# Hybrid attention block: the four single-purpose PSUM banks become one pool of four

## The chip, the cores and the metric

The kernel runs on one core of one Trainium2 chip. The metric is the device time of one launch in microseconds (us). TensorE (PE) does matrix products and transposes, PEld is its weight load, VectorE is DVE, ScalarE is ACT, GpSimd is POOL, and SyncE (SP) issues all loads.

## The reference

Two layers of a block run over 256 tokens of the stream x (width 1024) beside 256 context tokens. Each layer computes, from a normalised and modulated input h = norm(x)*(1+scale)+shift:

```python
p  = h @ w_in                               # keys, values, queries, gates, ...
y_na  = neighbourhood_attention(q, k, v, k_ctx, v_ctx, rpb)   # 8 heads of 64, bias table, mask
y_gm  = spatial_gating(gelu(u), gelu(v), ...)
y_mla = dense_attention(q_mla, [k_ctx; k_mla], [v_ctx; v_mla])  # 8 heads of 96, values of 64
y  = g0*(y_na @ na_w_o) + g1*(y_gm @ gm_w_o) + g2*(y_mla @ mla_w_o)  # g = sigmoid(p's gates)
x  = x + gt1 * (y @ w_out)
x  = x + gt2 * squared_relu_mlp(norm(x)*(1+scale)+shift)
```

In layer 0 the context tokens go through the same block (their attention sees context alone); in layer 1 only x does. The modulation vectors (shift, scale, gt) come from a product of a condition vector with w_mod.

## The kernel before

Activations lie transposed, 128 features by up to 512 tokens (256 of x, 256 of context; layer 1 works on 256). Every large product is made of three: weights and activations are each split into a rounded part and a rest (`split1`, L113, casts on ACT and subtracts on DVE), and `mm3` (L287 to L289) multiplies high by high, low by high and high by low into one PSUM tile.

PSUM has eight banks of 128 x 512 float32, and every PSUM tile is a whole bank. The function `psum` (L47) gives it a tag, and a tag owns a number of banks: "mm" four (all large products: `b_ps`, `gate`, `z`, `u`, `kv`, `qm`, `o_ps`, `f`), "s" two, "pt" one, "pv" one. What uses the last three:

- "s": the attention scores `S`, the transposes of keys and queries (`tr_ps`, `c_tr`, `h_tr`), the spatial gating product `sg`, and small ones (`st_ps`, `mod_t`, `rsum`).
- "pt": the transposed probabilities `pt`, and the sums of the modulation (`mod_ps` of `mod_quarter` and one of two in `mod_pooled`).
- "pv": the products of probabilities and values `pv` and `pvm`, the broadcast of the norms `rstd_b`, and the second sum of `mod_pooled`.

Attention is `soft_pv` (L427). It runs for four pairs of heads `j`, and in each for one or two streams and two blocks of 128 queries. For a block it forms the scores of both heads (two tiles `S`), then for each head: bias (DVE, neighbourhood attention on x only), row maximum (DVE, L445), exponential with its sum (ACT, L448, into one of two SBUF tiles `P`), reciprocal and scaling (DVE, L450, L451), transposes into `pt` (PE, L454) and a copy to SBUF (ACT, L456). After both blocks the products with the values go to `pv` (L460), which stays until `split_out` has read it (L423, L424), after all streams of the pair.

The order of the work is found when the program is built. A planner simulates the engines; each engine takes the ready instruction with the highest priority, which is its place in the program text, moved forward where `high_priority` says so. An instruction that writes a new tile can only be taken when a buffer of the tile's tag is free. The order so found is fixed: on the chip each engine works its list off from front to back and waits where an input or a buffer is late.

To give PE work beside the softmax, products of `gate` and `z` are spread over it. Each score product is recorded in `marks`, and `paced` (L305) lets the i-th group of three products (one `mm3`) go into the list only behind the score product that its share names, with the first `FREE` = 10 or `FREE2` = 36 groups free. Neighbourhood attention spreads 4 chunks of 12 groups in layer 0 and 6 in layer 1; the dense attention (MLA) spreads 96 groups.

Of the kernel before, what the change touches and what calls it, by code (L numbers as in the profile page):

```python
# [7 lines left out]
F32 = mybir.dt.float32  # L8
# [18 lines left out]
def hybrid_block_kernel(tc, a, out):  # L27
# [3 lines left out]
    mm = nc.tensor.matmul  # L31

    from contextlib import ExitStack, nullcontext
    with ExitStack() as es:
        def pool(name, bufs=1, **kw):
            return es.enter_context(tc.tile_pool(name=name, bufs=bufs, **kw))
# [8 lines left out]
        pp = pool("ps", space=PSUM)  # L45

        def psum(tag, name):  # L47
            return pp.tile([128, 512], F32, tag=tag, name=name, bufs={"mm": 4, "s": 2, "pt": 1, "pv": 1}[tag])


        def g2(name, dt=F32R):
# [88 lines left out]
        def mod_finish(ps, w, dsts, modT, bmod, streams):  # L140

            t = tmp2("mod_sb")
            vec.tensor_copy(t[:, :w], ps[:, :w])
            pst = psum("s", "mod_t")
            for i in range(w // 128):
                nc.tensor.transpose(pst[:, i * 128:(i + 1) * 128], t[:, i * 128:(i + 1) * 128], ident)
            for i in range(w // 128):
                v4 = pst[:, i * 128:(i + 1) * 128].rearrange("p (j r) -> p j r", j=4)
                for v in range(streams):
                    o, b = dsts(modT[:, v, :], i), dsts(bmod, i)  # L150
                    i0 = v4[:, :, v]
                    if len(o.shape) == 3:
                        i0 = i0.rearrange("p (a b) -> p a b", a=2)
                    vec.tensor_tensor(out=o, in0=i0, in1=b, op=ALU.add)

        def mod_quarter(l, q, modT, bmod, streams):

            ps = psum("pt", "mod_ps")
            for kb in range(4):
                for kk in range(2):  # L160
                    raw = g2("rawm", F32)
                    nc.sync.dma_start(out=raw, in_=a["wmod1"][l, q, kb][:, kk * 512:kk * 512 + 512])
                    mod_cols(ps, raw, 0, 128, 2 * kb + kk)
                yield
            mod_finish(ps, 128, lambda m, i: m[:, 0:16].rearrange("p (a c) -> p a c", a=2)[:, :, 2 * q:2 * q + 2], modT,
                       bmod, streams)

        def mod_group(l, g, modT, bmod, streams):
            ps = psum("mm", "mod_ps")
            for k in range(KC):  # L170
                raw = load(a["wmod"][l, g - 2, k])
                mod_cols(ps, raw, 0, 256, k)
                yield
            mod_finish(ps, 256, lambda m, i: m[:, 8 * g:8 * g + 8].rearrange("p (j i) -> p j i", i=2)[:, :, i], modT, bmod,
                       streams)
# [371 lines left out]
        for l in range(L):  # L547
# [192 lines left out]
            for j in range(4):  # L740
# [6 lines left out]
                pv = psum("pv", "pv")  # L747
# [94 lines left out]
            for j in range(4):  # L842
                pv = psum("pv", "pvm")
# [226 lines left out]
```

## Time and profile before

| | |
|---|---|
| median of 3 runs (lowest, highest) | 1402.77 us (1400.9, 1403.62) |
| profiled execution: time, span | 1402.83 us, 1400.8 us |
| PE busy, weight loads | 1370.2 us (98%), 1161.8 us |
| DVE, ACT, POOL busy | 957.4, 704.7, 56.9 us |
| granted TensorE clock | 1.000 |
| matmuls | 8438 |
| DMA | 210.61 MB, mean 150 GB/s |

The span is the time from the first to the last instruction of the profiled execution; its whole time is 2.03 us longer. Busy is the union of an engine's instructions, so a PE at 98% stands still for 30.6 us in the span. In a row of the timeline the number in square brackets is how long the engine sat idle before the row and what ended that.

### The profile page before, as it was taken

To read this page: it belongs to the slowest core of one execution; us is meant where nothing else is said; L and a number is where in the kernel's file an instruction comes from. 1 tells how busy PE (TensorE), PEld (TensorE's weight loads), DVE (VectorE), ACT (ScalarE), POOL (GpSimd) and SP (SyncE) were. 2 spreads that over 40 slices of the span, in tenths; PEclk is the share of its full clock that TensorE was granted. 3 is DMA by queue.
4 is the path that set the end of the run, shared out by engine and by line. 5 is a ranking of instruction groups with operands and counts; after the bars stand their busy time and mean duration, and the time that the engine had idled before them with its cause. 6 is when DMAs were issued, how large, how long until landed. Compare 5 with 4: busy or idle time off the path is not lost.

```text
span 1400.8 us, 22572 instructions
## 1 busy us (share of the span) xinstructions
PE 1370.2 (98%) x8438; PEld 1161.8 (83%) x8438; DVE 957.4 (68%) x2071; ACT 704.7 (50%) x1440; POOL 56.9 (4%) x35
## 2 busy tenths in 40 slices
PE   6999999999999999999999999999999999999999
PEld 4788767777676789988888888988888878999998
DVE  4666477665563558899766665786787766877775
ACT  3466256443453346623324233566676665656654
POOL 0110000110000000000000000011002100000000
PEclk9999999999999999999999999999999999999999
DMA  9423542234313465665555552443543434566664
GB/s 331 142 84 106 187 150 90 71 105 123 119 46 114 127 195 168 208 202 172 203 205 188 175 197 89 150 137 94 181 136 99 136 91 136 181 181 180 183 183 148
DMA packets 67214, 210.61 MB, mean 150 GB/s; under 512 B 8609, under 2 KB 9633, under 8 KB 67105
## 3 DMA queue, kind: packets, MB, share of 16 engines
q1 hardware_dynamic: 67104, 209.18, 46.6%
q8 instruction: 66, 1.08, 0.3%
q14 instruction: 44, 0.35, 0.1%
HBM read 208.10 MB, written 1.05 MB: 149 GB/s over the span
## 4 chain that ended last, share of the span: by engine, by line
PE 96%; DVE 1%; DMA 1%; ACT 1%; issue 0%; SPq 0%; POOL 0%; ACTq 0%; DVEq 0%
PE o_ps L287 8%; PE o_ps L289 8%; PE o_ps L288 8%; PE f L288 6%; PE f L287 6%; PE f L289 6%; PE gate L287 5%; PE gate L288 5%; PE gate L289 5%; PE b_ps L287 5%; PE b_ps L288 4%; PE b_ps L289 4%; PE pt L454 3%; PE S L417 2%; PE z L287 2%; PE z L289 2%
## 5 line engine op out<-in xcount | busy, mean ns | idle before, releaser
L115 ACT ACTIVATE wh<-raw 128x512 fp32r<-128x512 f32 (+1 forms) x570 | 353.1, 626 | 515.8 <-PE o_ps L288 179.7
L116 DVE TENSOR_TENSOR wl<-raw,wh 128x512 fp32r<-128x512 f32 (+1 forms) x570 | 385.8, 683 | 178.1 <-ACT wh L115 172.7
L289 PE MATMUL f<-hH,wl 128*128 128x258 f32 (+2 forms) x560 | 180.9, 324 | 0.1
L287 PE MATMUL f<-hH,wh 128*128 128x258 f32 (+2 forms) x560 | 180.4, 323 | 0.5 <-ACT wh L115 0.5
L288 PE MATMUL f<-hL,wh 128*128 128x258 f32 (+2 forms) x560 | 180.4, 324 | 0.2 <-DVE hL L277 0.2
L288 PE MATMUL o_ps<-aL,wh 128*128 128x256 f32 (+1 forms) x544 | 176.1, 327 | 0.0
L287 PE MATMUL o_ps<-aH,wh 128*128 128x256 f32 (+1 forms) x544 | 176.0, 328 | 0.0
L289 PE MATMUL o_ps<-aH,wl 128*128 128x256 f32 (+1 forms) x544 | 175.6, 328 | 0.0
L287 PE MATMUL gate<-hH,wh 128*128 128x512 f32 (+1 forms) x384 | 140.5, 366 | 0.0
L289 PE MATMUL gate<-hH,wl 128*128 128x512 f32 (+1 forms) x384 | 130.3, 339 | 0.0
L288 PE MATMUL gate<-hL,wh 128*128 128x512 f32 (+1 forms) x384 | 130.1, 339 | 0.0
L287 PEld LDWEIGHTS f<-hH,wh 128*128 128x128 f32 x560 | 106.0, 190 | 9.1 <-ACT wh L115 0.7
L289 PEld LDWEIGHTS f<-hH,wl 128*128 128x128 f32 x560 | 106.2, 190 | 8.5 <-DVE wl L116 0.3
L288 PEld LDWEIGHTS f<-hL,wh 128*128 128x128 f32 x560 | 105.9, 190 | 8.5 <-DVE hL L277 0.4
L287 PEld LDWEIGHTS o_ps<-aH,wh 128*128 128x128 f32 x544 | 102.7, 190 | 9.5 <-ACT aH L937 0.8
L288 PEld LDWEIGHTS o_ps<-aL,wh 128*128 128x128 f32 x544 | 103.1, 190 | 8.5
L289 PEld LDWEIGHTS o_ps<-aH,wl 128*128 128x128 f32 x544 | 102.7, 190 | 8.8
L288 PE MATMUL b_ps<-wl,hH 128*128 128x512 f32 (+2 forms) x288 | 108.8, 381 | 0.0
L289 PE MATMUL b_ps<-wh,hL 128*128 128x512 f32 (+2 forms) x288 | 106.3, 381 | 0.0
L287 PE MATMUL b_ps<-wh,hH 128*128 128x512 f32 (+2 forms) x288 | 103.7, 385 | 0.0
L200 DVE SCALAR_TENSOR_TENSOR macc<-rawx,sS,macc 128x512 f32<-128x512 f32 x112 | 78.9, 748 | 32.7 <-DMA rawx<-in_wmod_dram 32.4
L287 PEld LDWEIGHTS gate<-hH,wh 128*128 128x128 f32 x384 | 72.7, 189 | 15.9 <-issue 7.5
(229 smaller groups left out, 2481.3 us busy)
## 6 DMA issues: line engine op xcount, KB each, us to landing
raw<-in_wa_dram SPq DMA_DIRECT2D x147, 512.0 KB, 3.6
raw<-in_w_dram SPq DMA_DIRECT2D x68, 512.0 KB, 3.6
raw<-in_wb_dram SPq DMA_DIRECT2D x32, 512.0 KB, 3.3
raw<-in_wmod_dram SPq DMA_DIRECT2D x32, 512.0 KB, 3.4
rawx<-in_wmod_dram SPq DMA_DIRECT2D x32, 512.0 KB, 4.5
raw<-in_wo_dram SPq DMA_DIRECT2D x24, 512.0 KB, 3.6
rawm<-in_wmod_dram SPq DMA_DIRECT2D x32, 256.0 KB, 6.0
rawx<-in_wmod_dram SPq DMA_DIRECT2D x32, 256.0 KB, 4.2
```

What stands on the lines that cost most here:

```text
L115: act(out=wh[:, :width], in_=src, func=AF.Copy)
L116: vec.tensor_tensor(out=wl[:, :width], in0=src, in1=wh[:, :width], op=ALU.subtract)
L200: summed = vec.scalar_tensor_tensor(out=o, in0=src, scalar=s, in1=o, op0=ALU.mult, op1=ALU.add)
L287: mm(ps, lhsT=sh, rhs=mh, start=first, stop=False)
L288: mm(ps, lhsT=sh, rhs=ml, start=False, stop=False)
L289: mm(ps, lhsT=sl, rhs=mh, start=False, stop=last)
L417: return mm(s, lhsT=Q[h][0:96, q0:q0 + 128], rhs=K[h][0:96, k0:k0 + nk], start=True, stop=True)
L454: nc.tensor.transpose(pt[:, i * 128:(i + 1) * 128], P[:, i * 128:(i + 1) * 128], ident)
```

## The change

Every tag other than "mm" is replaced by one tag "side" with four banks. The four banks of "mm" stay. No instruction is added or removed in the program text; what can differ is which bank a tile gets and, by the planner, when.

```diff
         def psum(tag, name):
-            return pp.tile([128, 512], F32, tag=tag, name=name, bufs={"mm": 4, "s": 2, "pt": 1, "pv": 1}[tag])
+            if tag != "mm":
+                tag = "side"
+            return pp.tile([128, 512], F32, tag=tag, name=name, bufs=4)
```

## Rows read from the trace of the kernel before

**Rows 1.** The page: busy time, share, instructions; shares of the chain.
```profile
PE 1370.2 (98%) x8438; PEld 1161.8 (83%) x8438; DVE 957.4 (68%) x2071; ACT 704.7 (50%) x1440; POOL 56.9 (4%) x35
...
PE 96%; DVE 1%; DMA 1%; ACT 1%; issue 0%; SPq 0%; POOL 0%; ACTq 0%; DVEq 0%
```

**Rows 2.** Busy time by stretch: start:end, length, PE, PEld, DVE, ACT, POOL, clock, DMA.
```profile
181.00:190.00 9.00, 8.71 (x47) 5.41 (x46) 8.38 (x18) 5.76 (x11) 0.00 (x0) 1.00 0.64 231
190.00:257.00 67.00, 64.56 (x391) 45.74 (x391) 48.71 (x133) 43.25 (x114) 2.34 (x2) 1.00 0.27 86
257.00:332.00 75.00, 72.68 (x385) 58.13 (x382) 44.22 (x93) 31.97 (x67) 11.31 (x7) 1.00 0.35 105
332.00:452.00 120.00, 120.00 (x632) 84.35 (x630) 61.13 (x147) 54.43 (x132) 0.00 (x0) 1.00 0.30 96
600.00:1000.00 400.00, 400.00 (x1986) 336.88 (x1985) 289.89 (x551) 169.91 (x315) 12.43 (x6) 1.00 0.50 166
1010.00:1066.00 56.00, 51.52 (x371) 43.40 (x370) 42.62 (x104) 38.08 (x85) 0.00 (x0) 1.00 0.40 120
1108.00:1164.00 56.00, 52.99 (x355) 40.53 (x355) 33.23 (x73) 33.06 (x75) 0.00 (x0) 1.00 0.24 72
```

**Rows 3.** Waits of PE, whole span: us in total, times, longest.
```profile
PE mod_ps L137 <- DMA rawm<-in_wmod_dram: 11.9, 1, 11.9
PE pt L454 <- ACT PT L456: 2.9, 4, 0.7
PE pt L454 <- DVE P L451: 1.8, 2, 0.9
PE h_tr L794 <- DVE kml L798: 1.8, 1, 1.8
PE S L410 <- ACT P L448: 1.7, 2, 1.5
PE h_tr L794 <- ACT qml L796: 0.7, 2, 0.5
```

**Rows 4.** Timeline of ACT at the start of layer 1's neighbourhood attention.
```profile
1013.74 1.28 ACT L448 ACT_TABLE_LOAD   x1
1015.04 0.69 ACT L448 ACTIVATE P<-S,nm 128x512 f32<-128x512 f32 x1
```

**Rows 5.** Timeline of PE there: start, us, line, operation.
```profile
1015.87 0.50 PE L410 MATMUL S<-naK,naQ 128*128 128x512 f32 x1 [1.45 <-ACT P L448]
...
1019.76 0.60 PE L454 MATMUL pt<-ident,P 128*128 128x128 f32 x4
1021.05 0.66 PE L454 MATMUL pt<-ident,P 128*128 128x128 f32 x4 [0.69 <-ACT PT L456]
```

**Rows 6.** Timeline of ACT there, one head's exponential and copy.
```profile
1020.89 0.68 ACT L448 ACTIVATE P<-S,nm 128x512 f32<-128x512 f32 x1
1021.46 0.20 ACT L448 ACTIVATION_READ_ACCUMULATOR P<-S,nm 128x1 f32 x1
1021.74 0.60 ACT L456 ACTIVATE PT<-pt 128x512 f32<-128x512 f32 x1
```

**Rows 7.** Timeline of PE at the end of layer 1's dense attention.
```profile
1155.48 0.28 PE L289 MATMUL gate<-hH,wl 128*128 128x256 f32 x1
1155.60 0.28 PE L287 MATMUL gate<-hH,wh 128*128 128x256 f32 x1
...
1156.66 0.60 PE L454 MATMUL pt<-ident,P 128*128 128x128 f32 x4
1158.01 0.66 PE L454 MATMUL pt<-ident,P 128*128 128x128 f32 x4 [0.75 <-ACT PT L456]
1159.56 0.63 PE L454 MATMUL pt<-ident,P 128*128 128x128 f32 x4 [0.89 <-DVE P L451]
1160.87 1.95 PE L460 MATMUL pvm<-PT,vml 128*64 128x256 f32 x16 [0.69 <-ACT PT L456]
1163.30 0.66 PE L287 MATMUL z<-yml,wh 128*128 128x256 f32 x2 [0.48 <-ACT yml L423]
```

**Rows 8.** Instructions on the tile pt: durations ns min/median/max, first and last start.
```profile
L456 ACT ACTIVATE PT<-pt x96: 364/597/602, 190.3 to 1160.2; 128x512 f32<-128x512 f32 x64, 128x256 f32<-128x256 f32 x32
```

**Rows 9.** Timeline of PE at the start of layer 0: its longest gap there.
```profile
20.14 1.22 PE L247 MATMUL rstd_b<-diag,ones 128*128 128x256 f32 x2 [0.54 <-DVE diag L244]
```

**Rows 10.** Chain that ended last, in the feed-forward: start, us, what.
```profile
682.57 1.86 PE mod_ps L207 x32
```

## Prediction
> **What bounds the kernel now.** I read the page first: PE is busy for 1370.2 of 1400.8 us [rows 1], so 30.6 us of standstill is all that any change in the order of work can win, and the rest is PE's own work, which this change leaves as it is. The chain of waits on the page says the same: 96% of it is PE [rows 1]. The waits of PE come next. The largest, 11.9 us, is the first load of weights at the start [rows 3]; no bank has a part in it. Then come the stretches [rows 2]. PE does not stand still in the feed-forward of layer 0 and what surrounds it (400.00 of 400), nor in layer 0's dense attention (120.00 of 120). It loses 0.29 and 2.44 us in layer 0's neighbourhood attention, 2.32 us in the preparation of the dense one, 4.48 us in layer 1's neighbourhood attention and 3.01 us in layer 1's dense attention: 12.5 us in five stretches. That is the money on the table, less what is no bank's doing.
>
> Of those waits the reader should sort out which end because a bank comes free, and which because data arrive. "pt waits for ACT PT" is the next head's transposes standing behind the copy that empties the one bank for them (2.9 us in 4 waits). "S waits for ACT P" is a score product behind the exponential that empties one of two banks (1.7 us in 2). "h_tr waits for DVE kml" and "for ACT qml" are transposes behind the copies that empty those same two banks (1.8 and 0.7 us). All four [rows 3] sum to 7.1 us. "pt waits for DVE P" (1.8 us) is a wait for data, and no bank helps it.
>
> **What the change does, part by part.** Nothing is added to or taken from any engine's list: 8438 matmuls before, 8438 after. Only the planner's freedom changes, so each term is a wait that goes or comes.
>
> *Transposes of keys and queries* (2.5 us of waits). They run while no pair of heads is open, so four banks serve where two did. A head's copies must now be four heads late instead of two before PE stands. Bounds: 0 to 2.5 us won. I take 1.8, the one long wait; the two short ones may come back, since the copies set the rate of a dense burst in any case.
>
> *Scores* (1.7 us). The long one, 1.45 us, has a cause on the chip: ACT stood in a table load of 1.28 us just before the first exponential [rows 4], so both score banks were full when PE came with the third score [rows 5]. With a third and fourth bank (no value product is open yet) two more scores and their paced gate groups stand in PE's list before anything needs that exponential. Bounds 0 to 1.7; I take 1.45.
>
> *Transposed probabilities* (2.9 us). Two consecutive heads can now use two banks, if the pool has one. A copy of 0.60 us [rows 8] no longer stands between them. It doesn't have one always: while a pair is open its value product holds one bank, and two scores hold two more. Bounds 0 to 2.9; I take half, 1.4.
>
> *Value products.* Before, they had a bank of their own, which nobody contested. There are 16 of these tiles (four pairs, two attentions, two layers). In the pool the first product of each may find four banks taken and wait for the next copy or exponential to end. What such a wait costs is not in the trace; its nearest row is the 0.69 to 0.75 us that a transpose stands behind a copy [rows 5, 7]. Bounds 0 to 16 x 0.7 = 11.2 us lost. The planner sees it coming and puts gate groups in the place, as it does for 92 of the 96 heads' transposes [rows 3, 8], so I take 1.0 us, near the lower end.
>
> *The pace of the filling work.* A gate group may be issued only behind its score, so scores that run ahead drag the filling ahead. In layer 1's dense attention 96 - 36 = 60 groups hang on 16 scores, 3.75 a score; a product there starts every 0.12 us [rows 7], a group takes 0.36 us, and each score by which the scores lead more than before moves 1.35 us of filling away from the end of the phase, where PE already stands 0.75 + 0.89 + 0.69 + 0.48 = 2.81 us for want of it [rows 7]. The lead can grow by 0 to 2 scores: 0 to 2.7 us lost. I take one score, 1.35. In the other three attentions unpaced products of the next stage wait behind, so there it costs nothing; if that cover failed, the bound is the same 2.7 us in layer 1's neighbourhood attention.
>
> *Everything else.* At the start the modulation sums pass through one bank four times. After its first load PE's longest gap there is 0.54 us [rows 9]; the loads set the pace. I count 0, with 1 us either way. In the feed-forward the pooled sums fill their two banks in 1.86 us [rows 10], at a PE that has no gap [rows 2]: 0; without that cover it would be the same small wait of 0.7 us twice.
>
> Sum against the profiled execution: -1.8 - 1.45 - 1.4 + 1.0 + 1.35 = -2.3 us, 1402.83 - 2.3 = 1400.5 us. Against the median of 1402.77 it is the same -2.3, since that execution lies 0.06 us off it.
>
> **The Trainium skill.** On repeated gaps the trace shows four waits of about 0.7 us among 96 heads for the single transpose bank [rows 3, 8]. The Trainium skill, Perfetto Trace Analysis, section Identifying Performance Opportunities, reads consistent bubbles on the busiest engine as a sign that buffers in SBUF or PSUM run short. By that rule the sum would be that of rival A; four in 96 is hardly consistent, so the trace bears it out weakly, and it gets less chance than the forecast.
>
> **Rivals.** *A, the banks were the whole matter:* every one of the four bank waits goes and nothing comes in their place, -7.1 us, 1395.7 us. For it: those waits name banks, and PE's list can be filled freely while work is at hand. Against it: what PE gains in the middle of layer 1 it partly loses at the end, for the softmax chain is as long as before. The two SBUF tiles for probabilities are unchanged, so more scores don't make a faster chain: per head ACT still needs 0.68 + 0.20 + 0.60 = 1.48 us [rows 6].
>
> *B, scores crowd out the transposes (slower):* score products need only keys and queries, which are ready long before; transposes need a finished softmax. Whenever a bank comes free, a score is ready to take it. Before, scores could take two banks at most; now they can take all that the value product leaves, and a transpose that becomes ready must wait for an exponential to end, its own engine's next 0.68 + 0.20 us [rows 6]. It decides in layer 1, where filling is short: 8 blocks of two heads in each attention, 32 heads. If half of them stand 0.7 us, the length of such a wait today [rows 5], it costs 11.2 us, and with the 4.65 won above the time is 1402.8 + 11.2 - 4.65 = 1409.4 us. For it: PE has gaps there already. Against it: in these stretches a head has 56/16 = 3.5 us of PE time [rows 2] to ACT's 1.48, so the chain has slack before it is last. It wins from the point where the wait for a bank exceeds that slack, or where the gate groups are used up.
>
> *C, nothing:* the planner fills every one of these places now and the gaps are the chip's small deviations from its simulation, which appear elsewhere in the same amount. 1402.8 us, give or take 1.5.
>
> **How the numbers follow.** The forecast has a chance of 0.40, its own range 1398 to 1403.5; A 0.22; B 0.20; C 0.18. A change of under 0.2%, 2.8 us, can't be told from none in this kernel, so faster means below 1400.0 and slower above 1405.6. Nearly all of A is faster (0.21) and nearly half of the forecast (0.18): 0.39. The rest of the forecast (0.22) and C (0.17) are within: 0.39, and B with a trace of C makes 0.22 slower. The range runs from 1394.5, a little below A, to 1408, which leaves out half of B.
>
> **What would show it.** Right: the same number of matmuls, PE busy within 2 us of 1370; the wait of h_tr for kml gone, and the S wait beside the table load gone; pt's waits for ACT PT fewer; the stretch before layer 1's dense attention ends a little longer idle than 2.81 us. B shows as many waits of pt or pv for ACT P (L448) in layer 1, and the stretches of both attentions there longer than 56 us. The prediction is wrong if a stretch that has no PE idle now (feed-forward, layer 0's dense attention) changes its length, or if PE's busy time itself moves by more than its idle time: then the order of neighbouring products costs something that I have left out.

## The result

The change makes the kernel slower: 1440.89 us (median of 4 runs, 1437.09 to 1442.29) against 1403.19 us (4 runs), a ratio of 1.0263, 95% interval 1.0236 to 1.0291. The prediction was 1400.5 us with a range to 1408; the change is 38 us where 2.3 the other way were forecast.

The page after: busy time of the engines, and the chain of waits by engine, as in [rows 1].

```profile
PE 1377.9 (96%) x8438; PEld 1165.4 (81%) x8438; DVE 960.3 (67%) x2071; ACT 706.1 (49%) x1440; POOL 57.0 (4%) x35
...
PE 87%; DVE 5%; ACT 3%; DMA 3%; issue 1%; SPq 1%; POOL 0%; ACTq 0%; DVEq 0%
```

The number of instructions is unchanged. The span is 1438.8 us, 38.0 more than before. PE's idle time is 1438.8 - 1377.9 = 60.9 us against 30.6 (+30.3), and its busy time is 7.7 us longer. DVE and ACT, which do the softmax, now own 8% of the chain where they had 2%.

The waits of PE after, to be held against [rows 3]:

```profile
PE pt L456 <- DVE P L453: 16.3, 23, 2.0
...
PE pv L462 <- ACT PT L458: 5.7, 8, 0.8
PE pvm L462 <- ACT PT L458: 4.9, 7, 0.7
...
PE pt L456 <- ACT PT L458: 2.1, 3, 0.8
```

The waits that were to go are gone or fewer: `h_tr` behind `kml` and the score behind the table load no longer appear, and `pt` behind the copy fell from 2.9 to 2.1 us. What came in their place is, but for 0.4 us, no wait for a bank. The transposes wait for the scaled probabilities (16.3 us in 23 waits, before 1.8 in 2), and the value products for the last copy (10.6 us in 15, before 1.9 in 3):

```profile
PE pv L460 <- ACT PT L456: 1.2, 2, 0.7
...
PE pvm L460 <- ACT PT L456: 0.7, 1, 0.7
```

Those are data at the end of the softmax: PE's list holds nothing else to do while it runs. The one wait that may be for a bank is a transpose behind an exponential (`pt` behind `P` of ACT, 0.4 us, in layer 0).

Where the 38.0 us lie can be read from landmarks in the two timelines. The first product of the keys starts at 25.6 us (before 23.8): 1.8. From there to the first output product of layer 0 (500.8 us before, 527.5 after) 24.9 us are added; from there to the first output product of layer 1 (1188.4 and 1226.4) 11.3 us; from there to the end nothing. The stretches with attention, columns as in [rows 2], from the first score to just behind the last value product, the first one up to the next attention's first score:

```profile
176.50:338.00 161.50, 144.58 (x790) 107.28 (x789) 101.38 (x247) 82.89 (x193) 14.02 (x8) 0.98 0.30 93
338.00:470.00 132.00, 124.62 (x650) 86.98 (x649) 64.25 (x151) 55.84 (x133) 0.00 (x0) 1.00 0.29 92
...
1035.70:1100.00 64.30, 55.62 (x383) 46.58 (x382) 45.09 (x109) 38.89 (x88) 0.00 (x0) 0.97 0.34 105
...
1142.00:1202.00 60.00, 53.60 (x355) 40.59 (x354) 33.87 (x73) 33.65 (x77) 0.00 (x0) 1.00 0.22 68
```

PE stands for 7.38 us in layer 0's dense attention, where it had no gap, for 8.68 us in layer 1's neighbourhood attention (before 4.48) and for 6.40 in its dense attention (before 3.01). The first stretch holds the neighbourhood attention of layer 0 and the preparation of the dense one: 16.92 us, where the three stretches of [rows 2] that cover it had 5.05.

**The new order.** The timeline of PE after, in layer 1's neighbourhood attention, scores and what follows them:

```profile
1068.55 0.50 PE L412 MATMUL S<-naK,naQ 128*128 128x512 f32 x1
...
1069.12 0.39 PE L412 MATMUL S<-naK,naQ 128*128 128x512 f32 x1
...
1073.52 1.22 PE L456 MATMUL pt<-ident,P 128*128 128x128 f32 x8 [0.91 <-DVE r L452]
1074.49 0.48 PE L412 MATMUL S<-naK,naQ 128*128 128x512 f32 x1
...
1075.04 0.39 PE L412 MATMUL S<-naK,naQ 128*128 128x512 f32 x1
...
1078.80 1.30 PE L456 MATMUL pt<-ident,P 128*128 128x128 f32 x8 [0.28 <-DVE r L452]
1080.79 1.95 PE L462 MATMUL pv<-PT,vna 128*64 128x256 f32 x16 [0.69 <-ACT PT L458]
1082.66 0.50 PE L412 MATMUL S<-naK,naQ 128*128 128x512 f32 x1
```

Both scores of a block come first, then nothing of attention until both transposes, and only behind these the next block's scores; at the end of a pair they stand even behind the whole value product. A block takes 1074.49 - 1068.55 = 5.94 us, the pair's second 1082.66 - 1074.49 = 8.17, and in them PE stands for 0.91 + 0.28 + 0.69 = 1.88 us. Before, both scores of the next block stood ahead of the first transposes there (the third score of the attention is at 1015.87, the first transposes at 1019.76 [rows 5]), and then one score of a later block followed each head's transposes:

```profile
1031.56 0.66 PE L454 MATMUL pt<-ident,P 128*128 128x128 f32 x4
1031.97 0.48 PE L410 MATMUL S<-naK,naQ 128*128 128x512 f32 x1
...
1033.59 0.60 PE L454 MATMUL pt<-ident,P 128*128 128x128 f32 x4
1033.95 0.48 PE L410 MATMUL S<-naK,naQ 128*128 128x512 f32 x1
...
1035.92 0.60 PE L454 MATMUL pt<-ident,P 128*128 128x128 f32 x4
```

In that order PE had no gap from 1027.58 to 1053.01 us. After the change, DVE and ACT show the chain that has to run to its end in each block:

```profile
1069.42 0.79 DVE L445 TENSOR_TENSOR S<-S,bias 128x256 f32<-128x256 f32 x2
...
1070.12 1.28 DVE L447 TENSOR_REDUCE nm<-S 128x1 f32<-128x512 f32 x2
...
1071.58 0.68 ACT L450 ACTIVATE P<-S,nm 128x512 f32<-128x512 f32 x1
...
1072.24 0.69 ACT L450 ACTIVATE P<-S,nm 128x512 f32<-128x512 f32 x1
...
1073.48 0.49 DVE L453 TENSOR_SCALAR P<-P,r 128x512 f32<-128x512 f32 x1
...
1074.24 1.19 ACT L458 ACTIVATE PT<-pt 128x512 f32<-128x512 f32 x2 [0.70 <-PE pt L456]
```

The start shows the same rule without any attention. Before, the first modulation products (`mod_ps`) ran ahead of the norm's sums (`st_ps`), which stand earlier in the text:

```profile
11.92 0.65 PE L137 MATMUL mod_ps<-rawm,sS 128*32 128x128 f32 x6 [11.92 <-DMA rawm<-in_wmod_dram]
12.50 1.01 PE L237 MATMUL st_ps<-ones,acc 128*128 128x1 f32 x4
```

After, PE stands until the sums, then for the broadcast, and only then begins `mod_ps`:

```profile
13.07 1.01 PE L239 MATMUL st_ps<-ones,acc 128*128 128x1 f32 x4 [13.07 <-DVE gq L598]
16.14 1.22 PE L249 MATMUL rstd_b<-diag,ones 128*128 128x256 f32 x2 [2.06 <-DVE diag L246]
17.15 0.86 PE L239 MATMUL st_ps<-ones,acc 128*128 128x1 f32 x4
17.94 3.19 PE L139 MATMUL mod_ps<-rawm,sS 128*32 128x128 f32 x50
```

Both readings suggest theory T (turns): the planner hands the banks of one tag out in the order in which the text first writes its tiles, even if a later writer is ready and a bank is free. At the start `mod_ps` is the fourth writer of its tag, so a bank is free for it from the beginning. Three tags were three separate queues, and scores could pass the transposes; one tag is one queue.

### The profile page after: what moved, and what is told of

It is laid out like the page before. It is cut to its first block, busy times and chain, and to the rows that moved or that the text cites. A ratio compares the mean times of both kernels' runs of the same rounds, so it can differ in the third digit from the quotient of the medians.

```text
span 1438.8 us, 22590 instructions
## 1 busy us (share of the span) xinstructions
PE 1377.9 (96%) x8438; PEld 1165.4 (81%) x8438; DVE 960.3 (67%) x2071; ACT 706.1 (49%) x1440; POOL 57.0 (4%) x35
## 4 chain that ended last, share of the span: by engine, by line
PE 87%; DVE 5%; ACT 3%; DMA 3%; issue 1%; SPq 1%; POOL 0%; ACTq 0%; DVEq 0%
PE o_ps L289 8%; PE o_ps L291 8%; PE o_ps L290 8%; PE f L290 6%; PE f L291 6%; PE f L289 6%; PE b_ps L289 4%; PE b_ps L291 4%; PE b_ps L290 4%; PE gate L289 4%; PE gate L290 4%; PE gate L291 4%; PE pt L456 2%; PE S L419 2%; PE z L289 2%; PE z L290 2%
## 5 line engine op out<-in xcount | busy, mean ns | idle before, releaser
L289 PE MATMUL gate<-hH,wh 128*128 128x512 f32 (+1 forms) x384 | 137.2, 357 | 0.0
L447 DVE TENSOR_REDUCE nm<-S 128x1 f32<-128x512 f32 (+1 forms) x96 | 56.1, 598 | 62.4 <-PE S L419 39.0
```

The lines of the kernel that those rows point to most:

```text
L289: mm(ps, lhsT=sh, rhs=mh, start=first, stop=False)
L447: vec.tensor_reduce(out=nm, in_=s[:, :nk], axis=AX.X, op=ALU.max, negate=True)
```

## The experiments

T had two rivals. C (capacity): four shared banks are too few because a value product holds one. P, of the prediction: scores crowd out the transposes.

**e1, the order alone, on the banks of before.**

```diff
-                        marks.append(score[hh](s[:, :nk], q0, k0, nk).ins)
+                        with tc.issue_after(turn[0]) if turn[0] else nullcontext():
+                            marks.append(score[hh](s[:, :nk], q0, k0, nk).ins)
 ...
+                            if i == 0 and hh == 1:
+                                turn[0] = tr.ins          # second head's first transposition
 ...
+                            if v == 0:
+                                turn[0] = m.ins           # a pair's first value product
```

> The kernel before with its own banks for s, pt and pv, but each score product is put behind the previous block's second transposition in PE's list, and behind the first value product where a pair's first stream has ended. Nothing else. Theory T (turns: the planner hands a tag's banks out in the order of the program, so in one pool a score waits until the transposes and the value product that stand before it in the text have their banks): this order alone makes the loss, so 1435 to 1441 us (the start, some 2 us of the 38, is not copied). Theory C (capacity: the four shared banks are too few because the value product holds one and scores take the rest): banks are as before, so 1401 to 1407 us. Theory P, of the prediction (scores crowd out transposes): scores come later here, never earlier, so no loss, 1401 to 1407 us.

Measured: 1457.65 us, ratio 1.0396 (1.0379 to 1.0413). The banks are those of before and nothing is crowded, so neither C nor P makes this loss; order alone loses more than the whole change. That it loses 17 us more than the change T had not expected. The waits of PE in this run suggest the reason, which e9 tests:

```profile
PE pt L457 <- ACT PT L461: 26.0, 39, 0.9
```

With no other work left, both heads' transposes come at once, and here they have one bank; in the pool they have two (2.1 us of that wait).

**e2 to e4, two of the three users pooled at a time.** Each is the kernel before with only `psum` changed (shortened here):

```diff
-bufs={"mm": 4, "s": 2, "pt": 1, "pv": 1}[tag]
+tag = {"s": "spt", "pt": "spt"}.get(tag, tag);   bufs={"mm": 4, "spt": 3, "pv": 1}[tag]     # e2
+tag = {"s": "spv", "pv": "spv"}.get(tag, tag);   bufs={"mm": 4, "spv": 3, "pt": 1}[tag]     # e3
+tag = {"pt": "ptpv", "pv": "ptpv"}.get(tag, tag); bufs={"mm": 4, "ptpv": 2, "s": 2}[tag]    # e4
```

> Scores (2 banks) and transposed probabilities (1) become one pool of three, the value products keep their own bank. Theory T: a score waits for the transposes before it but no longer for the value product; the softmax still drains in each block, though not at the end of each stream: 1415 to 1430 us. Theory C: the value product takes nothing from the pool, so most of the loss goes: 1403 to 1410 us. Theory P: scores and transposes still compete, so nearly all of the loss stays: 1435 to 1441 us.

> Scores (2 banks) and value products (1) become one pool of three, the transposed probabilities keep their own bank. Theory T: a score waits only where a value product stands before it, once per stream: 1410 to 1425 us. Theory C: the value product holds one bank of three, two are left for scores as before, so 1403 to 1408 us. Theory P: transposes can't be crowded out, 1401 to 1407 us.

> Transposed probabilities and value products become one pool of two, scores keep their two banks. Theory T: transposes and value products come in the order of the text in any case, so attention loses nothing; at the start the modulation sums now stand behind the norm's broadcast, up to 2 us: 1402 to 1407 us. Theory C: an open value product leaves one bank of two, as before: 1401 to 1407 us. Theory P: the same. All three agree here; a loss of more than 6 us would speak against all of them.

Measured: e2 1427.67 us (ratio 1.018, 1.0165 to 1.0195), e3 1459.96 us (1.0408, 1.0382 to 1.0435), e4 1406.82 us (1.0036, 1.0021 to 1.0051). e2 fell where T put it. e4 as well: where the text's order and the work's order agree, pooling costs little, 4.0 us in all. Its first `mod_ps` stands behind the broadcast, at 15.88 us instead of 11.92, and the first product of the keys comes 0.8 us later. e3 lies 35 us above T's range, and no theory expected it. In its rows of layer 1's neighbourhood attention all four scores of a pair stand behind the value product of the pair before, which is T's order, and then four heads' transposes follow with no score between them. They pass through a single bank: `pt` waits 14.4 us for copies (22 waits) and 13.6 us for probabilities (15). The clock was granted least of these four (0.987), and PE is busy for 1393.2 us, which is 23.0 of the 54.5 us by which the span is longer than before. No run takes these parts one by one.

**e5 and e6, scores ahead in the text.** The scores of block b+1 are written ahead of the softmax of block b, in the pool (e5) and on separate banks (e6):

```diff
-                    S = []
-                    for hh in range(2):
-                        s = psum("s", "S")
-                        marks.append(score[hh](s[:, :nk], q0, k0, nk).ins)
-                        S.append(s)
+                    S = ready.pop(0)                      # written by the block before
+                    at += 1
+                    if at < len(blocks):
+                        ready.append(scores(*blocks[at], marks))
```

> The changed kernel with its one pool of four, and the text of the attention put in another order: the scores of the next block (two tiles) are written ahead of the softmax of this one, across the pairs of heads too. Theory T: scores now have their turn before the transposes, the softmax no longer drains between blocks, and most of the 36 us of attention come back: 1400 to 1412 us. Theory C: two more scores want banks of the same four, so it is as slow or slower: 1436 to 1450 us. Theory P: scores crowd out transposes more than before: slower than 1441 us.

> The same order of the text with the banks of the kernel before (two, one, one). Theory T: with two banks of their own the scores could already run one block ahead as each exponential freed a bank; only their rank beside the transposes changes: 1399 to 1407 us. Theories C and P: the same. It is the control for the run of the pooled one: if both are equal, the pool itself is worth nothing.

Measured: e5 1414.10 us (ratio 1.0079, 1.0064 to 1.0095), e6 1403.89 us (1.0008, 0.9998 to 1.0017). The same pool of four, with two more scores wanting its banks, is 27 us faster than the change, for another order of the text. C and P expected it slower. It misses T's range by 2 us, and 12 us remain. In layer 1 next to nothing remains of the attention's loss (57 and 56 us for its two attentions, 56 each before [rows 2]); the first output product of layer 0 is already 11.2 us late.

**e7, three banks instead of four.**

```diff
-            return pp.tile([128, 512], F32, tag=tag, name=name, bufs=4)
+            return pp.tile([128, 512], F32, tag=tag, name=name, bufs=4 if tag == "mm" else 3)
```

> The changed kernel with a pool of three banks instead of four. Theory T: the turns are what costs, not the number of banks; a block needs two scores and then two transposes, and with a value product open two are left: 1440 to 1460 us, the loss grown by less than half. Theory C: a quarter fewer banks where banks are the limit: the loss at least doubles, over 1475 us. Theory P: the same as C.

Measured: 1455.72 us (ratio 1.0378). A quarter fewer banks adds 15 us to 38, as T said; C wanted more than a doubling. The number of banks counts too, but less than the order.

**e8, without the pace.**

```diff
-FREE = 10
-FREE2 = 36
+FREE = 400
+FREE2 = 400
```

> The changed kernel with the groups of gate and z products not tied to score products any more (all of them free). Theory T: in attention PE waits for a softmax chain that is longer than the work at hand; the filling is only used up earlier, so 1432 to 1450 us. A rival to it, the pace (the filling is there but its turn has not come, since scores are late): most of the loss comes back, under 1415 us.

Measured: 1485.22 us (ratio 1.0585), outside both ranges. The rival is refuted: with the pace gone the loss grows, so the filling was not held back but short. T's size was too small. PE is busy 1403.4 us there, 25.5 more than in the changed kernel, at a mean granted clock of 0.975: with the filling spent early PE stands longer at a stretch (the longest wait of `pt` is 3.1 us, in the changed kernel 2.0), and more of the work then runs at the lower clock.

**e9, the order alone, with two banks for a block's transposes.** e1 with the pools of e4.

> The run that put each score product behind the previous block's transposes and value product, with transposed probabilities and value products in one pool of two (as in the run that pooled those two). Scores keep two banks of their own. Theory T: this is the changed kernel's order in attention with the two banks for a block's transposes that its pool has there, and without pooled scores: 1436 to 1448 us, and the 17 us by which the first such run lay above the changed kernel go. Theory O (another order, found by chance, costs it): no relation, it stays near 1458 us.

Measured: 1442.63 us (ratio 1.0282, 1.0266 to 1.0298), 1.7 us from the changed kernel, although its scores have two banks of their own and share with nobody; theory O falls. In layer 1's neighbourhood attention the same two blocks' first scores are 5.94 us apart as well (1068.37 and 1074.31). The order plus that second transpose bank gives the change's time. Over the whole span its waits are divided otherwise (transposes behind the copy 10.2 us, for the scaled probabilities 11.1), so it is the total that agrees and not each wait.

**e10 to e12, what is left over and the start.** In e10 (pool) and e11 (separate banks), both with scores ahead, each stream's value products take a tile of their own. e12 is the changed kernel with the first modulation quarter ahead of the norms.

```diff
+                pv = psum("pv", pvname)
 ...
-                        m = mm(pv[64 * hh:64 * hh + 64, v * NX:(v + 1) * NX], ...
+                        m = mm(pv[64 * hh:64 * hh + 64, 0:NX], ...
 ...
+                act(out=H, in_=pv[:, 0:NX], func=AF.Copy)
+                vec.tensor_tensor(out=Lo, in0=pv[:, 0:NX], in1=H, op=ALU.subtract)
 ...
+        for _ in first[0]:                                # e12
+            pass
         pb0 = psum("pv", "rstd_b")
```

> The pooled kernel with scores written one block ahead, and the value products of each stream take a tile of their own that is read and closed at once (before, one tile stays open over both streams of layer 0; 8 more copies and subtractions of half the width). Theory T: what was left there (12 us, all of it in layer 0) is the bank held over the second stream: layer 0's loss of 11 us shrinks to under 4, in all 1402 to 1408 us. If the tile held is not the cause: 1412 to 1417 us.

> The same text with the banks of the kernel before: the control. The bank for value products is free anyway when the next stream wants it, so only the extra copies could show, beside PE: 1401 to 1407 us.

> The changed kernel, with the sums of the first modulation quarter written ahead of the norm's sums. Theory T: they have their turn for a bank first again, so PE starts on them when the first weights land, near 12 us, and the first product of the keys comes up to 1.8 us earlier: 1438 to 1441 us, at most 2 us under the changed kernel.

Measured: e10 1414.32 us (ratio 1.0079), e11 1404.29 (1.0007), e12 1441.53 (1.027). The tile that stays open is not what is left in e5. In e12 the modulation does have its turn first, at 11.95 us, but now both sums and broadcasts queue behind all of it, and the first product of the keys comes at 29.49 us, 3.9 us later than in the changed kernel. My expectation of up to 1.8 us gained was wrong: a single queue at the start delays one or the other. The whole takes as long as the changed kernel within the spread of the runs.

**e13 and e14, the turn of the value products.** e13 is e5's order with one more block of scores written ahead of each stream's value products (the line that does it); e14 is e5's text on the banks of e2.

```diff
+                emit(2)                                   # up to two blocks of scores stand ready
                 for i, kt in enumerate(kts):
```

> The pooled kernel with scores one block ahead, and at the end of a stream the scores of one more block are written before the value products. Theory V (what is left of the loss is the value product's turn: the next scores stand behind it, and PE, its paced filling used up, waits for the copy before it): PE's waits of value products for the copies fall from 12.0 us to under 5 and the time from 1414 to 1402 to 1409 us. Theory C (four banks are too few for two blocks of scores and a value product): more scores want banks, so no gain or a loss, 1412 to 1425 us.

> Scores and transposed probabilities in one pool of three, the value products with a bank of their own, scores written one block ahead. Theory V: no score stands behind a value product, so the 12 us go: 1401 to 1407 us. Theory C: three banks for two blocks of scores and the transposes are fewer than the four before: 1414 us or more.

Measured: e13 1418.88 us (ratio 1.0116), e14 1431.92 (1.021). The waits of PE, first in e5, then in e13, then in e14:

```profile
PE pv L479 <- ACT PT L475: 8.0, 9, 1.4
PE pvm L479 <- ACT PT L475: 4.0, 5, 1.2
PE pt L473 <- ACT PT L475: 2.4, 5, 0.5
...
PE pt L473 <- DVE P L470: 2.0, 3, 0.9
```

```profile
PE pt L478 <- ACT PT L480: 5.1, 9, 1.0
PE pt L478 <- DVE P L475: 4.3, 5, 1.2
...
PE pv L485 <- ACT PT L480: 0.7, 1, 0.7
PE pvm L485 <- ACT PT L480: 0.7, 1, 0.7
```

```profile
PE pt L472 <- ACT PT L474: 16.0, 28, 1.0
```

In e13 the wait did what theory V said (12.0 us to 1.4), the time did not. 5.0 us came back at the transposes, and PE's idle time fell by 3.4 us only, from 1411.3 - 1371.1 = 40.2 to 1419.1 - 1382.3 = 36.8. PE's busy time rose by 11.2 us, and some of layer 1 ran at a lower clock (0.93 granted from 1119 to 1190 us), so the time of this run does not weigh V alone. In e14 the value products wait for 1.9 us in all, and the transposes stand behind each other's copies instead. A reading that fits, though no run isolates it: scores written ahead take the banks before the transposes in the queue, which is what P described, by turn and not by race. So V is not shown as the cause of the last 12 us: where its wait goes, another comes. A shortage of banks for two blocks of scores fits e13 and e14, but e10 gives it no support, and which it is stays open.

## Why the prediction was wrong

**The step that failed** is the one on which the terms for the scores and for the pace rest, and rival B with them: that a score may take any bank as soon as one is free (in B's words, "Whenever a bank comes free, a score is ready to take it"). The banks of one tag go by turns. The lead of the scores over the transposes was to grow by 0 to 2 scores, 1 taken; it shrank from a block's two scores to none. I weighed the number of banks in every term and their order in none. Before, scores and transposes had separate tags, so its trace could not show them in one queue.

The price was missed with it. The prediction set 3.5 us of PE time per head against ACT's 1.48 us alone and saw slack. Without a lead a block waits for the whole chain from its first score to its last copy. In the rows above that is 1074.24 + 1.19 - 1068.55 = 6.9 us, about as long as the 2 x 3.5 = 7.0 us of PE time for a block, so work that is missing beside it becomes a gap. The cover that was to make this free in three of the four attentions, products of the next stage, was not there: PE stands for 16.92 us against 5.05 in layer 0's first stretch, 7.38 against 0 in its dense attention and 8.68 against 4.48 in layer 1's neighbourhood attention. A changed length of layer 0's dense attention was one of the prediction's own signs of being wrong.

**Point by point.** The long wait of `h_tr` (1.8 us) is gone as forecast; with the shorter ones `h_tr` waits 1.5 us in all where it waited 2.8. The table-load term (1.45 us) came true in name only. No score waits there, because the third score now stands behind the transposes; but PE stands for 0.52 + 0.66 + 0.37 = 1.55 us just behind the same table load (1041.46 to 1043.38 us), for inputs of the `z` products that ACT and DVE finish late. The `pt` term (1.4 of 2.9) gave 0.8 us. The value products' wait, 1.0 us taken and 11.2 the bound, grew from 1.9 to 10.6 us. That the bound held is luck: it was worked out for a wait for a bank, and in e1, where the value products keep a bank of their own, they wait for 6.3 + 4.8 = 11.1 us. What they wait for is the last copy, with no filling in PE's list beside it. The start, counted at 0 with 1 us either way, took 1.8. Rival B's direction was right and both attentions of layer 1 are longer, as it said, but its mechanism was not: the transposes wait for data (16.3 us), and at most the one wait of 0.4 us is for a bank that a score holds. One of the sums is off by a hundredth: B's chance of 0.20 and C's 0.01 make 0.21 for slower, not 0.22.

**The busy time** was to stay within 2 us of 1370 and rose by 7.7. The page's clock line hides it; stretches of 10 us in the changed kernel show it, and a value product there:

```profile
190.00:200.00 10.00, 7.25 (x44) 4.21 (x45) 4.04 (x10) 3.34 (x8) 0.00 (x0) 0.85 0.58 186
...
240.00:250.00 10.00, 9.07 (x46) 5.91 (x44) 3.81 (x12) 3.64 (x11) 0.00 (x0) 0.83 0.00 0
```

```profile
238.63 0.66 PE L456 MATMUL pt<-ident,P 128*128 128x128 f32 x4 [1.21 <-DVE P L453]
239.66 0.63 PE L456 MATMUL pt<-ident,P 128*128 128x128 f32 x4 [0.37 <-DVE P L453]
240.97 3.33 PE L462 MATMUL pv<-PT,vna 128*64 128x256 f32 x16 [0.69 <-ACT PT L458]
```

After three gaps in a row the sixteen products of `pv` take 3.33 us, where they take 1.95 at 2.4 GHz [rows 7]; the granted clock of that stretch is 0.83, a mix of 2.4 and 1.2 GHz. The mean over the span is 0.996. As an estimate, up to 1438.8 x 0.004 = 5.8 us of the 7.7 are what the lower level cost, if PE had work in all of that time; the rest is not explained. Gaps of this size don't always do it: `pv` at 1080.79 us above takes 1.95 us behind three gaps. The four runs of the changed kernel agree in kind: 1437.09 us at a mean of 0.999, 1442.29 at 0.993. The Trainium skill, TensorE: Matmul & The Clock Gate, section A second HAM failure mode: psum-queue depth-cycling, tells of short idles of PE between groups of matmuls, with banks cycled, that make the clock fall back; these rows agree, with the gaps' cause here the order and not the cycling itself.

## What to carry to other kernels

A pool's tag is a queue as well as a number of buffers: users that should pass one another need tags of their own, and users that come in text order anyway can share one at a small price (e4, 4.0 us). Before pooling, write down the order in which the text first writes the tiles and ask which later one runs ahead today. Where tiles must share, the order of the text is the lever: it was worth 27 us here, but no pooled order reached the kernel before, and neither version with separate banks (1.0008 and 1.0007) beat it.

## What was unexpected of the hardware

Gaps of 0.4 to 1.2 us in PE's stream can cost more than themselves, since the granted clock fell after some of them: 0.83 over 10 us in the changed kernel. In e8, with waits of `pt` of up to 3.1 us, the mean is 0.975 and PE's busy time 33 us longer than before (1403.4 against 1370.2).
